# Six fixed experts and ten ordered ones in a two-layer decoder: the unit of four at sixth place, the embedding's input on GpSimd's queue, the order read where it is first used

## The chip, the cores and the metric

The kernel runs on one core of one Trainium2 chip. The metric is the device time of one execution in microseconds (us). TensorE (PE), VectorE (DVE), ScalarE (ACT), GpSimd (POOL) and SyncE (SP) each run their own instruction stream in order and meet at semaphores; 16 DMA engines move data between HBM and the core's SBUF.

## What is computed

A decoder trunk of two layers over 256 tokens of width 1024, all in float32. Each layer is a mixer (layer 0: differential attention beside retention; layer 1: forgetting attention), a LayerNorm, a mixture of 16 experts of which each token takes two out of one group of four, a second LayerNorm, and a gated embedding of a per-layer input `p`:

```python
for i in range(DEPTH):
    h = layer_norm(DEEPNORM_ALPHA * x + mix, ...)
    ffn = grouped_moe(h, router_w, moe_w_gate[i], moe_w_up[i], moe_w_down[i])
    h = layer_norm(DEEPNORM_ALPHA * h + ffn, ...)
    x = h + jax.nn.sigmoid(h @ ple_gate[i]) * (p[i] @ ple_proj[i])

def grouped_moe(...):
    for e in range(N_EXPERTS):
        a = jax.nn.silu(h @ w_gate[e]) * (h @ w_up[e])
        y = y + dense_gate[..., e:e + 1] * (a @ w_down[e])
```

The experts' weights are most of the bytes: 16 experts of 6.3 MB in each of two layers, 201 MB of the 249 MB that are read.

## The kernel before

**Weights as a stream.** Every weight matrix is cut into chunks of 128 x 2048 floats (1 MB). `PLAN` lists all 236 chunks in the order of their use; `fetch` issues the next chunk on SP's DMA queue, as two halves of 512 KB into the pool `wp` (36 halves), or into a place of its own where `PLACES` names one ("split": four quarters in the pool of the split weights; 0, 1, 2: one of the big activation slots; "late": a tile of the layer). A half is loaded again when the matmuls that read it are done, in the order of their use. SP's stream holds hardly anything but these issues, so it runs ahead of the other engines by as much as the buffers allow. Each DMA raises one of eight semaphores, taken in turn (`DMAHW0` to `DMAHW7`, called lanes below), and an issue waits until the DMA that had its lane before has landed; so about eight of SP's transfers are under way at a time, and a DMA that ACT issues takes its turn among the same eight lanes. GpSimd's DMAs have semaphores of their own (`DMASW`).

**Experts in units.** A token's rows are gathered for an expert into 64 slots. `UNITS` pairs the experts, so that two of them share the 128 columns of the array; one unit holds four experts with 32 slots each (`LIGHT`). The units are worked through in this order, each by its place p from 0 to 6: `gate_up(p)` (matmuls of L1305), `act`, then `down(p - 1)` (L1335) and `scatter(p - 1)` (L1355). Before p = 0, `rows` (L1243) gathers the tokens; again after every odd p.

**Ranked experts.** Experts 0 to 3 (`FIXED`) are read where they lie. The other twelve are ranked by their number of tokens: the eight fullest become experts 4 to 11 and the four lightest 12 to 15, the unit of four. DVE finds the ranks in `order`, `values_load` (L1166) loads them into twelve registers of SP, and every later address of such an expert is made of one of these registers. If any expert has more tokens than slots (64, or 32 in the unit of four), a flag `fi` is 1, all engines take the branch of L1471 and `overflow` runs every expert once more in a loop.

**What the change touches.** `moe_steps` writes out the expert part of `PLAN`; its last two lines move the two chunks of `u` of experts 2 and 3 behind six later ones. `pT`, the transposed input `p` of the layer, is loaded on ACT's queue (L1479) into a slot in which a chunk of an earlier unit lies (`PLACES` 59), and read by the matmuls of `pp` (L1430 and L1422). `router`, `order`, `later` and `back` hold the router's small DVE operations.

Of the kernel before, what the change touches and what calls it, by code (L numbers as in the profile page):

```python
# [10 lines left out]
F32 = mybir.dt.float32  # L11
# [4 lines left out]
U32 = mybir.dt.uint32  # L16
AF = mybir.ActivationFunctionType
OP = mybir.AluOpType
# [8 lines left out]
ALPHA = 4.0 ** 0.25  # L27
# [8 lines left out]
PPAT = 5  # L36


FIXED, LIGHT = 4, 32
UNITS = [(0, 1), (2, 3), (4, 5), (12, 13, 14, 15), (6, 7), (8, 9), (10, 11)]  # L40
LAST = len(UNITS) - 1
PLACES = {20: "split", 21: "split", **{j + i: n for j in (14, 37, 58) for i, n in enumerate((0, 1, "late"))}, 79: 0, 22: 2}

# [6 lines left out]
def moe_steps(l):  # L50
    def down(p, fh=(0, 1)):
        return [("d", l, e, h) for h in fh for e in UNITS[p]]

    out = []
    for p in range(len(UNITS)):
        out += [(n, l, e, kh) for n in ("g", "u") for kh in range(2) for e in UNITS[p]]
        if p == 1:

            out += down(0) + down(1)
        elif p > 2:  # L60
            out += down(p - 1)
        if p == PPAT:
            out.append(("pp", l, 0))
    for fh in range(2):
        out += down(LAST, (fh,))
        if l == DEPTH - 1 and fh == 0:
            out += EARLY
    out.append(("pp", l, 1))

    i = out.index(("u", l, 2, 1))  # L70
    return out[:i] + out[i + 2:i + 8] + out[i:i + 2] + out[i + 8:]
# [162 lines left out]
def trunk(ctx: ExitStack, tc, w, xT_d, pT_d, prm_d, rows_d, rb_d, cst_d, e_d, dt_d, out):  # L234
    nc = tc.nc
# [10 lines left out]
    def bank(tag, dt=F32):  # L246
        return psum.tile([128, 512], dt, name=tag, tag=tag)
# [3 lines left out]
    pos = [0]  # L251
# [8 lines left out]
    ranked = {}  # L260

    def source(key, c):

        if key[0] in ("g", "u", "d") and key[2] >= FIXED:
            l = key[1]
            of = w[(l * NE + FIXED) * 6:(l + 1) * NE * 6].rearrange("(x j) p c -> x j p c", j=6)
            return of[bass.ds(ranked[l][key[2] - FIXED], 1), "gud".index(key[0]) * 2 + key[3], :, c]
        return w[AT[key], :, c]

# [801 lines left out]
    def router(l, lt, rstd, finish, keep, residual, two):  # L1071
# [69 lines left out]
        NS = NE - FIXED  # L1141
        tmp = two.tile([128, 512], F32, name="r_tmp", tag="a", bufs=1)
        key = tmp[:, 0:32].rearrange("p (i e) -> p i e", i=2)
        perm = tmp[:, 32:176].rearrange("p (r e) -> p r e", r=NS)
        prod = tmp[:, 176:464].rearrange("p (t r e) -> p t r e", t=2, r=NS)
        load = tmp[:, 464:480]
        far = tmp[:, 480:496].rearrange("p (i r) -> p i r", i=2)
        rank = tmp[:, 496:512].bitcast(U32).rearrange("p (i r) -> p i r", i=2)
        spos = keep.tile([128, 2, 16], F32, name="r_spos")

        def arranged(out, in_):
# [5 lines left out]
        def order(behind):  # L1157

            with tc.issue_after(behind):
                DVE.tensor_copy(load, cnt)  # L1160
                DVE.scalar_tensor_tensor(key[:, 0, 0:NS], load[:, FIXED:], 16.0, i16[:, 0:NS], op0=OP.mult, op1=OP.subtract)
            DVE.tensor_scalar(key[:, 1, 0:NS], key[:, 0, 0:NS], -1.0, None, op0=OP.mult)
            for i in range(2):
                DVE.max(out=far[:, i, :], in_=key[:, i, 0:NS])
                DVE.max_index(out=rank[:, i, :], in_max=far[:, i, :], in_values=key[:, i, 0:NS])
            _, ranked[l] = nc.values_load_multi_w_load_instructions(  # L1166
                rank[0:1].rearrange("p i r -> p (i r)")[:, 0:NS], engines=[mybir.EngineType.SP], min_val=0, max_val=NS - 1,
                skip_runtime_bounds_check_because="indices of the largest of so many")
            DVE.tensor_tensor(perm, i16[:, None, 0:NS].to_broadcast([128, NS, NS]),
                              rank.rearrange("p i r -> p (i r)")[:, 0:NS, None].to_broadcast([128, NS, NS]), op=OP.is_equal)  # L1170
            arranged(spos, pos)

        def later():

            ri = new([2], "r_ri")
            DVE.reciprocal(ri, rs)
            pr = new([2, 2], "r_pr")
            DVE.tensor_tensor(pr, m8[:, :, 0:2], ri[:, :, None].to_broadcast([128, 2, 2]), op=OP.mult)
            gsum = new([2], "r_gsum")
            DVE.tensor_tensor(gsum, pr[:, :, 0], pr[:, :, 1], op=OP.add)  # L1180
            DVE.reciprocal(gsum, gsum)
            DVE.tensor_tensor(pr, pr, gsum[:, :, None].to_broadcast([128, 2, 2]), op=OP.mult)
            e2 = eq.rearrange("p t j e -> p (t j) e")
            DVE.tensor_tensor(e2, e2, pr.rearrange("p t j -> p (t j)")[:, :, None].to_broadcast([128, 4, 16]), op=OP.mult)
            gate = keep.tile([128, 2, 16], F32, name="r_gate")
            DVE.tensor_tensor(gate, eq[:, :, 0, :], eq[:, :, 1, :], op=OP.add)
            sgate = keep.tile([128, 2, 16], F32, name="r_sgate")
            DVE.tensor_copy(sgate[:, :, 0:FIXED], gate[:, :, 0:FIXED])
            arranged(sgate, gate)

            cap = keep.tile([128, 16], F32, name="r_cap")
            DVE.memset(cap, float(CAP))
            DVE.tensor_scalar(cap[:, FIXED:], key[:, 1, 0:NS], far[:, 1, 3:4], None, op0=OP.is_ge)
            DVE.tensor_scalar(cap[:, FIXED:], cap[:, FIXED:], float(LIGHT - CAP), float(CAP), op0=OP.mult, op1=OP.add)

            fm = small.tile([1, 16], F32, name="r_fm")
            DVE.tensor_tensor(fm, load[0:1], cap[0:1], op=OP.is_gt)
            fi = keep.tile([1, 1], I32, name="r_fi")
            DVE.tensor_reduce(fi, fm, axis=AX.X, op=OP.max)
            return gate, sgate, cap, fi  # L1200

        return pos, spos, order, later, rest


    def moe(l, hT, n2, acc, keep, two, xs, residual, *lt):
            pos, spos, order, later, rest = router(l, *lt, keep, residual, two)
            gate = sgate = cap = fi = None
            g0, b0 = P_MG + 8 * l, P_MB + 8 * l
            xg, sl, aT, sT, gsl = {}, {}, {}, {}, {}
            last = []  # L1210
# [43 lines left out]

            def back(q, after=None):

                nonlocal gate, sgate, cap, fi
                if q == 0:
                    with tc.issue_after(after):
                        gate, sgate, cap, fi = later()  # L1260
                s32 = two.tile([128, 2, 4 * CAP], F32, name="sel", tag="a", bufs=1)
                select(q, s32)
                o = bank("w").rearrange("p (b t) -> p b t", b=2)
                og = bank("w")
                us = UNITS[2 * q:2 * q + 2]
                for b in range(len(us)):
                    for tt in range(2):
                        c = slice(b * 128, (b + 1) * 128)
                        PE.transpose(o[:, b, tt * 128:(tt + 1) * 128], s32[:, tt, c], ident)
                        PE.matmul(og[:, 16 * b:16 * b + 16], lhsT=s32[:, tt, c], rhs=sgate[:, tt, :],  # L1270
                                  start=tt == 0, stop=tt == 1, skip_group_check=True)
                st = two.tile([128, 2, 256], FR, name="sT")
                DVE.tensor_copy(st[:, 0:len(us)], o[:, 0:len(us)])
                sT[q] = st

                gg = two.tile([128, 2], F32, name="gg")
                if len(together(q)) < len(us):
                    for i in range(2):
                        r, c = slice(64 * i, 64 * i + 64), us[0][i]
                        DVE.tensor_scalar(gg[r], og[r, c:c + 19:18], 1.0 / ALPHA, None, op0=OP.mult)  # L1280
                else:
                    for b, es in enumerate(us):
                        n = 128 // len(es)
                        for i, e in enumerate(es):
                            r = slice(n * i, n * i + n)
                            DVE.tensor_scalar(gg[r, b:b + 1], og[r, 16 * b + e:16 * b + e + 1], 1.0 / ALPHA, None, op0=OP.mult)
                gsl[q] = gg

            def gate_up(p, between, amid=None):
# [70 lines left out]
            def overflow():  # L1360

                T = two.tile
                og = T([128, 2, 16], F32, name="og", tag="og", bufs=1)
                DVE.tensor_tensor(og, pos, cap[:, None, :].to_broadcast([128, 2, 16]), op=OP.is_gt)
                DVE.scalar_tensor_tensor(og, og, 1.0 / ALPHA, gate, op0=OP.mult, op1=OP.mult)
                id16 = T([128, 128], F16, name="id16", tag="id16", bufs=1)
                DVE.tensor_copy(id16, ident)

# [83 lines left out]
            for p in range(len(UNITS)):  # L1452
# [23 lines left out]
                    gb = broadcast()  # L1476
                if p == PPAT:
                    pT = slot(XSLOT[l][1], "pT", shape=(128, 2, S))
                    nc.scalar.dma_start(out=pT, in_=pT_d[l])  # L1479
                    ppT = keep.tile([128, 8, S], F32, name="ppT", tag="late")  # L1480
                    for o in pp(0, pT, ppT):
                        DVE.tensor_scalar(*o, 0.5, None, op0=OP.mult)
# [140 lines left out]
```

## Time and profile before

| | us |
|---|---|
| median of three runs | 758.33 |
| lowest and highest | 757.03 and 761.68 |
| the profiled execution's own time | 759.22 |
| span of its instructions | 757.2 |

The span is counted from the first to the last instruction of the program in the one execution that was profiled; 2.0 us of that execution's time lie around it. Its time is 0.9 us above the median. Times inside the profile are us from the start of the span. Of the engines, PE is busy for 95% of the span, DVE 42%, ACT 32%, POOL 6%; PE's busy time is modelled, so that a matmul that waits between its parts can look busy.

### The profile page before, as it was taken

To read this page: it belongs to the slowest core of one execution; us is meant where nothing else is said; L and a number is where in the kernel's file an instruction comes from. 1 tells how busy PE (TensorE), PEld (TensorE's weight loads), DVE (VectorE), ACT (ScalarE), POOL (GpSimd) and SP (SyncE) were. 2 spreads that over 40 slices of the span, in tenths; PEclk is the share of its full clock that TensorE was granted. 3 is DMA by queue.
4 is the path that set the end of the run, shared out by engine and by line. 5 is a ranking of instruction groups with operands and counts; after the bars stand their busy time and mean duration, and the time that the engine had idled before them with its cause. 6 is when DMAs were issued, how large, how long until landed. Compare 5 with 4: busy or idle time off the path is not lost. (4 is left out here: it accounts for less than half of the span.)

```text
span 757.2 us, 11670 instructions
## 1 busy us (share of the span) xinstructions
PE 718.0 (95%) x4126; PEld 426.9 (56%) x4126; DVE 321.0 (42%) x799; ACT 242.3 (32%) x507; POOL 44.5 (6%) x42
## 2 busy tenths in 40 slices
PE   6999999999999897999999999989999998799897
PEld 6977887435334232547989897763443432243367
DVE  6687777303102011218757666671221211020585
ACT  5557656101001010105667566451111100020441
POOL 3000101000000000004000000010000000000036
PEclk9999999999999999999999999999999999999999
DMA  8999883899999799999997437559999969999901
GB/s 285 376 408 408 325 295 123 329 410 415 407 409 414 255 409 409 408 403 409 408 410 289 137 141 281 187 179 371 413 411 409 414 247 344 407 409 409 395 37 56
DMA packets 70526, 250.82 MB, mean 331 GB/s; under 512 B 7835, under 2 KB 9408, under 8 KB 67776
## 3 DMA queue, kind: packets, MB, share of 16 engines
q1 hardware_dynamic: 70176, 249.51, 84.8%
q8 instruction: 34, 0.56, 0.3%
q10 hardware_dynamic: 288, 0.52, 0.3%
q14 instruction: 28, 0.23, 0.1%
HBM read 248.95 MB, written 1.05 MB: 330 GB/s over the span
## 5 line engine op out<-in xcount | busy, mean ns | idle before, releaser
L1305 PE MATMUL w<-wt,xg 128*64 128x512 f32 (+1 forms) x1024 | 204.3, 595 | 7.5 <-DMA wt<-in_w_dram 5.1
L1335 PE MATMUL w<-wt,aT 128*64 128x512 f32 (+1 forms) x512 | 129.8, 607 | 15.6 <-DMA wt<-in_w_dram 15.5
L1305 PEld LDWEIGHTS w<-wt,xg 128*64 128x64 f32 (+1 forms) x1024 | 63.3, 130 | 130.0 <-issue 106.4
L385 DVE TENSOR_TENSOR wlo<-wt,whi 128x512 fp32r<-128x512 f32 x145 | 106.4, 749 | 42.6 <-ACT whi L383 35.3
L383 ACT ACTIVATE whi<-wt 128x512 fp32r<-128x512 f32 x148 | 91.0, 629 | 63.4 <-PE acc L435 24.9
L1335 PEld LDWEIGHTS w<-wt,aT 128*64 128x64 f32 (+1 forms) x512 | 39.5, 132 | 96.6 <-issue 63.5
L1346 ACT ACTIVATE whi<-w,gg 128x512 fp32r<-128x512 f32 x28 | 19.3, 688 | 184.9 <-PE w L1335 166.4
L1312 DVE TENSOR_TENSOR a<-a,w 128x512 f32<-128x512 f32 x14 | 9.6, 687 | 140.8 <-PE w L1305 101.8
L435 PE MATMUL acc<-xh,whi 128*128 128x256 f32 x192 | 50.9, 290 | 5.4 <-ACT whi L383 5.4
L1347 DVE SCALAR_TENSOR_TENSOR wlo<-w,gg,whi 128x512 fp32r<-128x512 f32 x28 | 20.6, 746 | 73.0 <-ACT whi L1346 72.8
L435 PE MATMUL acc<-xh,wlo 128*128 128x256 f32 x192 | 50.7, 289 | 0.8 <-DVE wlo L385 0.8
L1311 ACT ACTIVATE a<-w 128x512 f32<-128x512 f32 x14 | 8.4, 597 | 119.0 <-PE w L1305 57.7
L435 PEld LDWEIGHTS acc<-xh,whi 128*128 128x128 f32 x192 | 37.4, 196 | 6.7 <-ACT whi L383 6.5
L377 POOL TENSOR_TENSOR lnrs<-lnve,mhalf 128x1 f32<-128x1 f32 x8 | 4.4, 546 | 589.3 <-DVE lnve L467 586.1
L435 PEld LDWEIGHTS acc<-xh,wlo 128*128 128x128 f32 x192 | 37.4, 195 | 1.5 <-DVE wlo L385 1.3
L421 PE MATMUL acc<-whi,xh 128*128 128x512 f32 x96 | 38.1, 396 | 0.0
L421 PE MATMUL acc<-whi,xl 128*128 128x512 f32 x96 | 38.0, 396 | 0.0
L421 PE MATMUL acc<-wlo,xh 128*128 128x512 f32 x96 | 37.1, 390 | 0.0
L435 PE MATMUL acc<-xl,whi 128*128 128x256 f32 x192 | 37.1, 286 | 0.0
L1253 ACT ACTIVATE xg<-w,prm 128x256 f32<-128x256 f32 (+1 forms) x32 | 15.5, 534 | 63.3 <-PE w L1243 63.2
L1320 DVE COPY aT<-w 128x512 f32<-128x512 f32 x14 | 9.7, 692 | 53.4 <-PE w L1335 40.0
L435 PEld LDWEIGHTS acc<-xl,whi 128*128 128x128 f32 x192 | 29.5, 195 | 0.0
(314 smaller groups left out, 1008.0 us busy)
## 6 DMA issues: line engine op xcount, KB each, us to landing
wt<-in_w_dram SPq DMA_DIRECT2D x406, 512.0 KB, 10.1
wt<-in_w_dram SPq DMA_DIRECT2D x21, 1024.0 KB, 10.9
wt<-in_w_dram SPq DMA_DIRECT2D x40, 256.0 KB, 5.7
x<-in_xT_dram SPq DMA_DIRECT2D x3, 256.0 KB, 5.8
dt<-in_dt_dram SPq DMA_DIRECT2D x1, 512.0 KB
tmp<-scr SPq DMA_DIRECT2D x1, 512.0 KB, 6.2
pT<-in_pT_dram ACTq DMA_DIRECT2D x2, 256.0 KB, 2.7
out_dram<-wt SPq DMA_DIRECT2D x2, 256.0 KB, 2.0
```

The costliest lines, as they stand in the source:

```text
L383: i = ACT.activation(hi, src, AF.Copy)
L385: return i, (eng or DVE).tensor_tensor(lo, src, hi, op=OP.subtract)
L421: PE.matmul(o, lhsT=wa[p], rhs=wb[q], start=start and i == 0, stop=stop and i == 2, skip_group_check=True)
L435: m = PE.matmul(outs[b], lhsT=ws[kk][i % 2][:, b * 128:(b + 1) * 128], rhs=x2[i // 2][:, kk, :], start=kk == 0 and b in first and i == 0, ...
L1253: ACT.activation(xt[:, k, 0:n], o[:, b, :], AF.Identity, bias=be, scale=g)
L1305: PE.matmul(o[m * i:m * i + m, :], lhsT=xg[p // 2][:, k, c:c + m], rhs=ws[i, k // 4][k % 4], start=k == 0, stop=k == 7)
L1311: ACT.activation(a, ps["g"], AF.Silu)
L1312: DVE.tensor_tensor(a, a, ps["u"], op=OP.mult)
L1320: DVE.tensor_copy(t.rearrange("p f s -> p (f s)"), pt)
L1335: PE.matmul(ob[nh][m * i:m * i + m, :], lhsT=aT[p][:, f, m * i:m * i + m], rhs=ws[i, f // 2][2 * (f % 2) + nh], start=f == 0, stop=f == 3)
L1346: last[:] = (ACT.activation(yh, ob[nh], AF.Copy, scale=gg), DVE.scalar_tensor_tensor(yl, ob[nh], gg, yh, op0=OP.mult, op1=OP.subtract))
L1347: DVE.scalar_tensor_tensor(yl, ob[nh], gg, yh, op0=OP.mult, op1=OP.subtract))
```

## The change

`FIXED` is 6 instead of 4, so ten experts are ranked: the six fullest of them are experts 6 to 11, the four lightest 12 to 15. The unit of four stands sixth (p = 5) instead of fourth (p = 3). `moe_steps` lists every unit's `d` chunks one unit later, from the first on, as `down` uses them. The registers of SP are loaded by a function that runs when the first ranked expert's address is made. The ranks get a tile of their own (`r_rank`), `cap` a corner of the temporary one, and the overflow's gate is made in `later` and no longer in the branch. `pT` is loaded on GpSimd's queue.

```diff
-FIXED, LIGHT = 4, 32
-UNITS = [(0, 1), (2, 3), (4, 5), (12, 13, 14, 15), (6, 7), (8, 9), (10, 11)]
+FIXED, LIGHT = 6, 32
+UNITS = [(0, 1), (2, 3), (4, 5), (6, 7), (8, 9), (12, 13, 14, 15), (10, 11)]
...
-        if p == 1:
-
-            out += down(0) + down(1)
-        elif p > 2:
+        if p:
             out += down(p - 1)
...
+            if callable(ranked[l]):
+                ranked[l] = ranked[l]()
             return of[bass.ds(ranked[l][key[2] - FIXED], 1), "gud".index(key[0]) * 2 + key[3], :, c]
...
-        perm = tmp[:, 32:176].rearrange("p (r e) -> p r e", r=NS)
-        prod = tmp[:, 176:464].rearrange("p (t r e) -> p t r e", t=2, r=NS)
+        perm = tmp[:, 32:32 + NS * NS].rearrange("p (r e) -> p r e", r=NS)
+        prod = tmp[:, 176:176 + 2 * NS * NS].rearrange("p (t r e) -> p t r e", t=2, r=NS)
...
-        rank = tmp[:, 496:512].bitcast(U32).rearrange("p (i r) -> p i r", i=2)
+        rank = keep.tile([128, 16], U32, name="r_rank")
...
-                DVE.max_index(out=rank[:, i, :], in_max=far[:, i, :], in_values=key[:, i, 0:NS])
-            _, ranked[l] = nc.values_load_multi_w_load_instructions(
-                rank[0:1].rearrange("p i r -> p (i r)")[:, 0:NS], engines=[mybir.EngineType.SP], min_val=0, max_val=NS - 1,
-                skip_runtime_bounds_check_because="indices of the largest of so many")
+                DVE.max_index(out=rank[:, i * (NS - 4):i * (NS - 4) + 8], in_max=far[:, i, :], in_values=key[:, i, 0:NS])
+            ranked[l] = lambda: nc.values_load_multi_w_load_instructions(
+                rank[0:1, 0:NS], engines=[mybir.EngineType.SP], min_val=0, max_val=NS - 1,
+                skip_runtime_bounds_check_because="indices of the largest of so many")[1]
...
+            DVE.tensor_copy(spos[:, :, 0:FIXED], pos[:, :, 0:FIXED])
             arranged(spos, pos)
...
-            cap = keep.tile([128, 16], F32, name="r_cap")
+            cap = tmp[:, 496:512]
...
-            return gate, sgate, cap, fi
+
+            beyond = prod.rearrange("p t r e -> p (t r e)")[:, 0:32].rearrange("p (t e) -> p t e", t=2)
+            DVE.tensor_tensor(beyond, pos, cap[:, None, :].to_broadcast([128, 2, 16]), op=OP.is_gt)
+            DVE.scalar_tensor_tensor(gate, beyond, 1.0 / ALPHA, gate, op0=OP.mult, op1=OP.mult)
+            return gate, sgate, fi
...
                 if p == PPAT:
                     pT = slot(XSLOT[l][1], "pT", shape=(128, 2, S))
-                    nc.scalar.dma_start(out=pT, in_=pT_d[l])
+                    nc.gpsimd.dma_start(out=pT, in_=pT_d[l])
```

Where the instructions stand is seen in the built programs. On SP's queue, at layer 0's expert part, the quarters `128x512` are the chunks of `u` of experts 2 and 3, `TENSOR_LOAD` is the load of the registers, and an `ISA` row makes an address from one. Before:

```order
L290 DMA wt<-in_w_dram 128x1024 x46
L290 DMA wt<-in_w_dram 128x2048 x3
L290 DMA wt<-in_w_dram 128x1024 x6
L290 DMA wt<-in_w_dram 128x512 x4
L1166 TENSOR_LOAD r_tmp
L290 DMA wt<-in_w_dram 128x512 x4
L290 DMA wt<-in_w_dram 128x2048
L290 DMA wt<-in_w_dram 128x1024 x2
L290 ISA
L290 DMA wt<-in_w_dram 128x1024
```

After the change, the same place:

```order
L289 DMA wt<-in_w_dram 128x1024 x46
L289 DMA wt<-in_w_dram 128x2048 x3
L289 DMA wt<-in_w_dram 128x1024 x6
L289 DMA wt<-in_w_dram 128x512 x8
L289 DMA wt<-in_w_dram 128x2048
L289 DMA wt<-in_w_dram 128x1024 x18
L1165 TENSOR_LOAD r_rank
L289 ISA
L289 DMA wt<-in_w_dram 128x1024
```

The load of the registers has moved behind 23 issues: the second four quarters, one chunk in a slot, and 18 halves.

On ACT's queue in layer 0, `pT` stands behind the `a` of the unit at p = 4 (with what each instruction waits for). Before:

```order
L1346 ACTIVATE whi<-w,gg 128x512 [waits PE_49] x2
L1253 ACTIVATE xg<-w,prm 128x256 [waits PE_49]
L1253 ACTIVATE xg<-w,prm 128x256
L1311 ACTIVATE a<-w 128x512 [waits DVE_49,PE_49]
L1479 DMA pT<-in_pT_dram 128x512 [waits DMAHW5_49,DMAHW7_49,DMAHW4_49,PE_49]
L1346 ACTIVATE whi<-w,gg 128x512 [waits PE_49,Activation_49] x2
```

After the change it stands on POOL's queue, behind the branch of the overflow and ahead of the LayerNorm's small operations:

```order
L1472 ISA [waits DMASW3_49,DMASW4_49,DMASW2_49,DMASW5_49,DMASW1_49,DMASW0_49]
L1472 UNCONDITIONAL_BRANCH
L1480 DMA pT<-in_pT_dram 128x512 [waits DMAHW5_49,DMAHW4_49,DMAHW7_49,DMASW0_49,PE_49]
L376 TENSOR_TENSOR lnrs<-lnve,mhalf 128x1 [waits DVE_49,Activation_49,Pool_49]
L376 TENSOR_TENSOR lnrs<-lnve,mhalf 128x1 [waits DVE_49]
```

It waits for PE's last read of its slot, as before, and its landing is told by a semaphore of GpSimd's (`DMASW0`).

On PE, at the end of layer 0's expert part, the last unit's `gate_up` is followed by the `down` of the unit before it. `64x512` are matmuls of a pair, `32x512` of the unit of four. Before:

```order
L1430 MATMUL w<-pT,wt 128x256 x8
L1305 MATMUL w<-wt,xg 64x512 x16
...
L1305 MATMUL w<-wt,xg 64x512 x16
L1335 MATMUL w<-wt,aT 64x512 x16
L1318 MATMUL w<-identr,a 128x128 x4
L1355 MATMUL acc<-whi,sT 128x512 x2
```

After the change:

```order
L1431 MATMUL w<-pT,wt 128x256 x8
L1309 MATMUL w<-wt,xg 64x512 x9
...
L1309 MATMUL w<-wt,xg 64x512 x16
L1339 MATMUL w<-wt,aT 32x512 x2
L1322 MATMUL w<-identr,a 128x128 x4
L1339 MATMUL w<-wt,aT 32x512 x30
L1359 MATMUL acc<-whi,sT 128x512 x2
```

The `down` that PE meets there is now that of the unit of four, which reads eight chunks instead of four.

## Rows read from the trace of the kernel before

**Rows 1.** The page: the GB/s that the DMA engines moved in 40 equal slices of the span (18.9 us each).

```profile
GB/s 285 376 408 408 325 295 123 329 410 415 407 409 414 255 409 409 408 403 409 408 410 289 137 141 281 187 179 371 413 411 409 414 247 344 407 409 409 395 37 56
```

**Rows 2.** The chain of work that ended last, merged: start, us, what. The last transfer in it, of layer 1's expert part.

```profile
704.72 9.53 DMA wt<-in_w_dram
```

**Rows 3.** PE in order of time: start, us, line, operation, tiles, shapes, number of instructions (two to a matmul in float32), and in brackets the idle time before and what ended it. The first expert matmul of each layer; then of layer 0 a half of `gate_up` and a `down` of a pair, `gate_up` and a part of `down` of the unit of four, and the last `down`; then the last `down` of layer 1.

```profile
131.96 1.51 PE L1305 MATMUL w<-wt,xg 128*64 128x512 f32 x6 [0.50 <-ACT xg L1253]
506.22 1.08 PE L1305 MATMUL w<-wt,xg 128*64 128x512 f32 x4 [0.50 <-ACT xg L1253]
...
177.14 7.09 PE L1305 MATMUL w<-wt,xg 128*64 128x512 f32 x32
192.33 7.04 PE L1335 MATMUL w<-wt,aT 128*64 128x512 f32 x32
202.93 13.93 PE L1305 MATMUL w<-wt,xg 128*32 128x512 f32 x126
261.86 6.39 PE L1335 MATMUL w<-wt,aT 128*32 128x512 f32 x24 [2.53 <-DMA wt<-in_w_dram]
334.98 8.11 PE L1335 MATMUL w<-wt,aT 128*64 128x512 f32 x30
714.29 7.31 PE L1335 MATMUL w<-wt,aT 128*64 128x512 f32 x16 [2.99 <-DMA wt<-in_w_dram]
```

**Rows 4.** Waits of SP's queue over the whole span: who waited for whom, us in total, times, the longest.

```profile
SPq L290 <- DMA pT<-in_pT_dram: 26.2, 2, 14.8
SPq L290 <- PE w L1305: 24.1, 44, 5.5
SPq L1166 <- DVE r_tmp L1165: 20.7, 2, 12.9
```

**Rows 5.** SP's queue in order of time, from four windows that hold two issues each: start of the first, us from there to the end of the second, line, tile, number of issues. Layer 0, layer 0, layer 1, layer 1.

```profile
118.50 14.91 SPq L290 DMA_DIRECT2D wt<-in_w_dram  x2
242.34 12.22 SPq L290 DMA_DIRECT2D wt<-in_w_dram  x2
498.06 10.47 SPq L290 DMA_DIRECT2D wt<-in_w_dram  x2
609.89 15.70 SPq L290 DMA_DIRECT2D wt<-in_w_dram  x2
```

**Rows 6.** The same view. The first two run from each layer's first expert weight over 124 issues; the other three over 24 issues of 512 KB or as many bytes: an undisturbed stretch, then layer 0 and layer 1 from the first issue of the second and fourth of rows 5.

```profile
49.02 193.65 SPq L290 DMA_DIRECT2D wt<-in_w_dram  x124
383.30 226.93 SPq L290 DMA_DIRECT2D wt<-in_w_dram  x124
199.14 29.70 SPq L290 DMA_DIRECT2D wt<-in_w_dram  x24
242.34 35.99 SPq L290 DMA_DIRECT2D wt<-in_w_dram  x24
609.89 39.90 SPq L290 DMA_DIRECT2D wt<-in_w_dram  x24
```

**Rows 7.** The view of the tile `pT`, over both layers: ACT's issue of its DMA (the times of the two issues stand behind the durations in ns), and the time from issue to landing.

```profile
L1479 ACTq DMA_DIRECT2D pT<-in_pT_dram x2: 339/358/377, 251.3 to 622.5; - x2
DMA to landing us min/median/max: 2.6/2.7/2.8
```

**Rows 8.** PE by line from 251.2 to 343.1, which is layer 0's expert part from the last read of the slot that `pT` takes: line, operation, tiles, shapes, number of instructions, busy us and mean ns of one, idle us before them and what ended it. The three groups that are left out are busy for 0.6 us or less each.

```profile
L1335 PE MATMUL w<-wt,aT 128*64 128x512 f32 (+1 forms) x160 | 39.2, 614 | 6.8 <-DMA wt<-in_w_dram 6.7
L1305 PE MATMUL w<-wt,xg 128*64 128x512 f32 x129 | 30.0, 596 | 3.0 <-DMA wt<-in_w_dram 2.2 <-PEq L1471 0.7
L1355 PE MATMUL acc<-whi,sT 128*128 128x512 f32 x13 | 4.7, 432 | 0.1
L1355 PE MATMUL acc<-wlo,sT 128*128 128x512 f32 x12 | 4.1, 429 | 0.0
L1430 PE MATMUL w<-pT,wt 128*128 128x256 f32 x16 | 3.7, 384 | 0.0
L1318 PE MATMUL w<-identr,a 128*128 128x128 f32 x12 | 2.0, 287 | 0.0
L1243 PE MATMUL w<-sel,n 128*128 128x128 f16 x32 | 2.0, 219 | 0.0
```

**Rows 9.** Stretches of 10 us: PE, PEld, DVE, ACT and POOL busy (instructions), the granted TensorE clock, the DMA engines' busy share, GB/s. Four of layer 0's expert part, one of layer 1's.

```profile
120.00:130.00 10.00, 8.95 (x93) 7.40 (x92) 7.00 (x36) 8.33 (x22) 2.84 (x3) 1.00 0.16 51
250.00:260.00 10.00, 9.23 (x50) 2.34 (x45) 0.69 (x1) 0.00 (x0) 0.00 (x0) 1.00 0.58 179
260.00:270.00 10.00, 8.02 (x29) 2.58 (x30) 1.71 (x3) 1.38 (x2) 0.00 (x0) 0.83 1.01 398
280.00:290.00 10.00, 7.31 (x32) 2.24 (x32) 0.64 (x1) 0.00 (x0) 0.00 (x0) 1.00 1.03 408
620.00:630.00 10.00, 9.77 (x53) 2.77 (x50) 0.69 (x1) 0.00 (x0) 0.00 (x0) 1.00 0.45 141
```

**Rows 10.** DVE in order of time in layer 0's router: the last index search, one of the four large operations of `arranged`, and the selection that PE waits for.

```profile
131.66 0.17 DVE L1165 FIND_INDEX8 r_tmp<-r_tmp 128x8 uint32<-128x12 f32 x1
134.30 0.45 DVE L1153 TENSOR_TENSOR r_tmp<-r_tmp,r_gate 128x288 f32<-128x288 f32 x1
135.28 0.76 DVE L1229 TENSOR_TENSOR sel<-stay,r_pos 128x256 f32<-128x256 f32 x2
```

More of the change, by code (lines that the diff above doesn't have):

```diff
@@ L1164, in order @@
                 DVE.max(out=far[:, i, :], in_=key[:, i, 0:NS])
-                DVE.max_index(out=rank[:, i, :], in_max=far[:, i, :], in_values=key[:, i, 0:NS])
-            _, ranked[l] = nc.values_load_multi_w_load_instructions(
-                rank[0:1].rearrange("p i r -> p (i r)")[:, 0:NS], engines=[mybir.EngineType.SP], min_val=0, max_val=NS - 1,
-                skip_runtime_bounds_check_because="indices of the largest of so many")
+                DVE.max_index(out=rank[:, i * (NS - 4):i * (NS - 4) + 8], in_max=far[:, i, :], in_values=key[:, i, 0:NS])
+            ranked[l] = lambda: nc.values_load_multi_w_load_instructions(
+                rank[0:1, 0:NS], engines=[mybir.EngineType.SP], min_val=0, max_val=NS - 1,
+                skip_runtime_bounds_check_because="indices of the largest of so many")[1]
             DVE.tensor_tensor(perm, i16[:, None, 0:NS].to_broadcast([128, NS, NS]),
-                              rank.rearrange("p i r -> p (i r)")[:, 0:NS, None].to_broadcast([128, NS, NS]), op=OP.is_equal)
+                              rank[:, 0:NS, None].to_broadcast([128, NS, NS]), op=OP.is_equal)
+            DVE.tensor_copy(spos[:, :, 0:FIXED], pos[:, :, 0:FIXED])
             arranged(spos, pos)
@@ L1206, in moe @@
             pos, spos, order, later, rest = router(l, *lt, keep, residual, two)
-            gate = sgate = cap = fi = None
+            og = sgate = fi = None
             g0, b0 = P_MG + 8 * l, P_MB + 8 * l
@@ L1255, in back @@
             def back(q, after=None):
-                nonlocal gate, sgate, cap, fi
+                nonlocal og, sgate, fi
                 if q == 0:
                     with tc.issue_after(after):
-                        gate, sgate, cap, fi = later()
+                        og, sgate, fi = later()
                 s32 = two.tile([128, 2, 4 * CAP], F32, name="sel", tag="a", bufs=1)
@@ L1263, in back @@
                 o = bank("w").rearrange("p (b t) -> p b t", b=2)
-                og = bank("w")
+                sg = bank("w")
                 us = UNITS[2 * q:2 * q + 2]
@@ L1269, in back @@
                         PE.transpose(o[:, b, tt * 128:(tt + 1) * 128], s32[:, tt, c], ident)
-                        PE.matmul(og[:, 16 * b:16 * b + 16], lhsT=s32[:, tt, c], rhs=sgate[:, tt, :],
+                        PE.matmul(sg[:, 16 * b:16 * b + 16], lhsT=s32[:, tt, c], rhs=sgate[:, tt, :],
                                   start=tt == 0, stop=tt == 1, skip_group_check=True)
@@ L1279, in back @@
                         r, c = slice(64 * i, 64 * i + 64), us[0][i]
-                        DVE.tensor_scalar(gg[r], og[r, c:c + 19:18], 1.0 / ALPHA, None, op0=OP.mult)
+                        DVE.tensor_scalar(gg[r], sg[r, c:c + 19:18], 1.0 / ALPHA, None, op0=OP.mult)
                 else:
@@ L1285, in back @@
                             r = slice(n * i, n * i + n)
-                            DVE.tensor_scalar(gg[r, b:b + 1], og[r, 16 * b + e:16 * b + e + 1], 1.0 / ALPHA, None, op0=OP.mult)
+                            DVE.tensor_scalar(gg[r, b:b + 1], sg[r, 16 * b + e:16 * b + e + 1], 1.0 / ALPHA, None, op0=OP.mult)
                 gsl[q] = gg
@@ L1362, in overflow @@
                 T = two.tile
-                og = T([128, 2, 16], F32, name="og", tag="og", bufs=1)
-                DVE.tensor_tensor(og, pos, cap[:, None, :].to_broadcast([128, 2, 16]), op=OP.is_gt)
-                DVE.scalar_tensor_tensor(og, og, 1.0 / ALPHA, gate, op0=OP.mult, op1=OP.mult)
                 id16 = T([128, 128], F16, name="id16", tag="id16", bufs=1)
```

## The prediction

> **What bounds the kernel now.** I read the DMA engines' GB/s by slices first, then the chain that ended last, then SP's waits, and last PE inside the expert parts. An undisturbed stream moves 408 to 414 GB/s; inside the expert parts there are dips that no other engine's work explains: 123 in the slice from 114 us, 255 from 246, 247 from 606 [rows 1]. The chain ends in weight transfers, and behind the last of them PE's last `down` starts after 2.99 us of waiting for it [rows 2, 3]. PE looks busy, but from 251.2 to 343.1 in layer 0 its work is four `down` at 7.04 (28.2), four halves of `gate_up` at 7.09 (28.4) [rows 3], and shorter groups of 16.5 plus at most 1.8 [rows 8]: 74.9 of 91.9 us, so 17.0 us are waits, whole or inside matmuls. In layer 1 the same work lies between 622.5 [rows 7] and 714.29 + 7.31 = 721.6 [rows 3]: 99.1 us, so 24.2 us of waits. The weight stream sets the end of both expert parts, and a hole in it comes back there us for us until these 17 and 24 us are used up. A hole's owner is read from SP: it waited 12.9 us for the register load, up to 14.8 us for `pT`, and 44 times for PE, 5.5 us at most [rows 4].
>
> **The register load.** In layer 0 two neighbouring issues of SP take 14.91 us from 118.50 on [rows 5]; between them stands the load, which waits for the index search that ends at 131.83 [rows 10]. Meanwhile the stream falls to 51 GB/s [rows 9]. Behind the load stand three chunks whose places are free (the second four quarters and two others), 3.1 MB, 7.7 us at 408 GB/s: the most that can be won. A second count: the first 124 issues of the expert part end at 242.67 in layer 0, 110.71 us after PE's first expert matmul, and at 610.23 in layer 1, 104.01 us after it [rows 3, 6]. In layer 1 the load's hold (10.47 us, to 508.53) ends where PE starts to free buffers, just after 506.22 [rows 3, 5], so it costs nothing there. The difference, 6.7 us, is what the load costs layer 0; I take it, between 0 and 7.7, since it is measured on the same 124 issues. After the change the load stands 23 issues later; the ranks are long known there, and the load with one issue takes 1.6 us (131.83 to 133.41), with eight transfers of 29.70/23 = 1.29 us under way [rows 6]: nothing. So **−6.7 us, in layer 0 alone**.
>
> **`pT`.** On ACT's queue its DMA takes one of eight lanes in program order, but is issued only when PE has read its slot, at 251.3 and 622.5 [rows 7]; the SP issue next on that lane waits for it. Two issues take 12.22 and 15.70 us [rows 5], and the stream falls to 179 and 141 GB/s [rows 9]. Over 24 issues that is 35.99 and 39.90 us against 29.70 [rows 6]: 6.3 and 10.2 us, of which `pT`'s own 256 KB (0.64 us at 408 GB/s) stay. On GpSimd's queue it has a semaphore that no SP instruction waits for: **−5.7 us in layer 0, −9.6 in layer 1**. The bounds are zero and the full 6.3 and 10.2. These holds end with PE and not with the stream, so layer 1's lead of 6.7 us is eaten by a hold that is 3.5 us longer; undoing one hold alone would therefore be worth less than its share.
>
> Is there cover? In layer 0, 6.7 + 5.7 = 12.4 come off 17.0 us of PE's waits, 4.6 are left; in layer 1, 9.6 off 24.2, 14.6 are left. Next late is the stream again.
>
> GpSimd's transfer is not in this trace. ACT's landed in 2.6 to 2.8 us [rows 7]. In the new order the slot is freed in the middle of p = 5's first half, and PE wants `pT` at `pp(0)`, about half a `gate_up` half, one more, a `down`, transposes, scatter and the gather later: 3.5 + 7.1 + 7.0 + some 5 = 23 us, which is hidden at 2.7 us and up to 23. I take zero. ACT waits for nothing of `pT`, so there is no gain beside the lane. On POOL behind it stand only the LayerNorm's small operations at the layer's end.
>
> **The unit of four at sixth place.** Its PE work is a pair's: 13.93 us against 2 x 7.09 [rows 3]. Its weights are 24 chunks (25 MB) where a pair's are 12, 61 us of stream. What moves is where PE waits for them: its `down` (eight chunks, 20.5 us of stream, 7 us of PE) now stands just ahead of the last `down`, so PE meets a lump of some 6 to 8 us of waits at the end. What that costs is the clock: a wait of 2.53 us in the four's `down` came with a granted clock of 0.83 over its 10 us, while 280 to 290, where PE was busy for 7.31 of 10 in many short waits, had 1.00 [rows 3, 9]. 0.83 is 3.4 us at the lower level (1.2 GHz) in ten, 1.7 us of work lost; it counts only behind the last transfer of an expert part. Bounds: the last `down`s took 8.11 for 30 instructions and 7.31 for 16, against 6.6 and 3.5 at 0.22 each [rows 3], so if the new order took their waits away, −1.5 and −3.8; if each layer loses what that dip cost and 0.7 of a gap more, +2.4. In layer 1 three chunks of `ppg` (7.7 us) stand between the lump and the last `down` and cover it. I take half the upper figure for layer 0 and zero for layer 1, nearest to the 0.83 row: **+1.2 us**.
>
> [...]
>
> **Router and the rest.** In place of operations on 288 elements (0.45 us each, four of them [rows 10]) stand such on 200, and a small copy and two small operations are added at about 0.17 each, the last two behind the selection: between −0.5 and +0.5, taken as zero. The overflow's gate leaves a branch that isn't taken. Buffers are freed in the order of use as before; `d` is now listed a unit later from the first on, so that SP waits for PE at other issues. It waited 44 times already [rows 4] and the slices from 530 to 606 still show 411 to 414 GB/s [rows 1]: eight transfers under way (10.3 us) cover a wait of 5.5. Zero, with the rival below.
>
> **Sum** on the profiled execution: 759.2 − 6.7 − 5.7 − 9.6 + 1.2 = 738.4; that execution is 0.9 above the median, so **737.5 us**. With every term at its better end (7.7, 6.3, 10.2, −5.3) it is 728.8, with every one at its dearer end, short of a rival, some 744. A difference within 1% (7.6 us) cannot be told from none by a measurement of this kernel.
>
> **Rivals.** *PE becomes the bound in layer 0.* Only 4.6 us of its waits are left by the sum. If the lump stands at the lower clock for longer (a `down` at half speed is 7 us dearer in each layer; layer 1's cover takes most of its), the time is 737.5 + 7 = 744 to 748. For it: 0.83 and 2.5 us waits already; against it: at most one such dip in a stretch now. Chance 0.12.
>
> *SP waits for PE instead.* With `d` listed later, issues wait for reads by PE that themselves wait for weights. If one wait in each layer outlasts the 10.3 us under way by the longest seen, 5.5 [rows 4], the time is 737.5 + 11 = 748. Against it: the full slices from 530 on. Chance 0.05.
>
> *The change doesn't do what it says:* the stream still halts for `pT`. Then layer 0's lead of 6.7 us is eaten at the hold as in layer 1, and the time is the old one with the four's cost, 757 to 760. The holes are waits with idle DMA engines (share 0.45 to 0.58 [rows 9]), and the program shows no SP issue on GpSimd's semaphore. Chance 0.04.
>
> The Trainium skill ("DMA: Bandwidth & Descriptors", section "Rules for kernel authors") says that spreading DMAs over SP, ACT and GpSimd brings no bandwidth, since all run on the same 16 engines, and only saves issue time. By that alone `pT` would be worth nothing and the time would be this rival's; the idle share in the rows says that the gain here is an order of waiting, not bandwidth.
>
> *Slower:* `pT` by GpSimd comes late. PE then stands at `pp(0)`, in order ahead of p = 6. The 23 us of cover and the waits left (4.6 and 14.6) hide it up to 28 and 38 us; each us beyond is paid. At 47 us it is 19 + 9 = 28 more, 766, slower by 1%. No row speaks for a 256 KB transfer of 47 us; the nearest is 2.7. Chance 0.03.
>
> **Numbers.** The forecast has 0.76, in 730 to 744. With the two rivals of 0.12 and 0.05 in part, the range **730 to 747** holds a little over 8 in 10. Faster by over 1% (below 750.7): 0.76 + 0.12 + 0.04 less some doubt in all of them, **0.87**; within 1%: **0.09**; slower: **0.04**.
>
> **What would show it.** In the changed profile SP has no wait of 12 us or more in either expert part except for PE; the first 124 issues end about 104 us after the first expert matmul in both layers; GB/s stays near 408 from 140 to the end of layer 0's weights; its last `down` ends near 332 instead of 343.1; `pT` is issued by POOL and PE doesn't wait for it; PE's waits for weights lie in the four's `down` with a clock below 1.00 there; the span is some 736. Wrong would be: a new hole of the stream with PE behind SP's waits, a wait of PE for `pT`, or a last `down` that starts long after its weights have landed.

## The result and the profile after

The changed kernel takes 734.79 us (median of four runs, 732.79 to 737.25) beside 758.66 for the kernel before: ratio 0.968, 95% interval 0.964 to 0.9725. The profiled execution is the longest of the four, 737.25 us with a span of 735.4; it stands against 759.22 and 757.2.

The page of the changed kernel, engines' busy time and GB/s by slices (18.4 us each):

```profile
PE 711.4 (97%) x4126; PEld 427.8 (58%) x4126; DVE 320.7 (44%) x805; ACT 242.4 (33%) x507; POOL 45.8 (6%) x44
...
GB/s 287 354 410 408 371 263 261 322 389 415 410 408 414 408 407 410 408 377 401 409 408 301 128 141 282 185 189 333 412 413 409 412 411 408 406 410 408 391 4 58
```

Of the three dips of [rows 1], two are gone: the slices that answer to 255 and 247 show 408 to 414. The third is shallower, 261 where it was 123. The lower slices from 74 to 147 us, around the start of the expert part, stay. Waits of SP's queue, whole span: who waited for whom, us in total, times, the longest.

```profile
SPq L289 <- PE w L1309: 64.9, 52, 9.5
SPq L289 <- PE w L1339: 17.6, 23, 3.6
```

Against [rows 4] the lines for `pT` and for the register load are missing, and the waits for PE's reads in `gate_up` have grown from 24.1 to 64.9 us, the longest from 5.5 to 9.5. SP's first 124 issues from each layer's first expert weight, as in [rows 6]: start, us, line, tile, number.

```profile
49.77 185.53 SPq L289 DMA_DIRECT2D wt<-in_w_dram  x124
372.67 224.81 SPq L289 DMA_DIRECT2D wt<-in_w_dram  x124
```

And PE in order of time, as in [rows 3]: the first expert matmul of each layer, layer 0's last `down`, layer 1's.

```profile
132.04 3.65 PE L1309 MATMUL w<-wt,xg 128*64 128x512 f32 x16 [0.50 <-ACT xg L1257]
493.93 3.65 PE L1309 MATMUL w<-wt,xg 128*64 128x512 f32 x16 [0.50 <-ACT xg L1257]
...
323.19 8.11 PE L1339 MATMUL w<-wt,aT 128*64 128x512 f32 x30
691.81 8.39 PE L1339 MATMUL w<-wt,aT 128*64 128x512 f32 x16 [3.22 <-DMA wt<-in_w_dram]
```

The 124 issues now end 103.3 us (235.30 − 132.04) and 103.6 us (597.48 − 493.93) after the first expert matmul; before it was 110.7 and 104.0. From the first expert matmul to the end of the last `down`, layer 0 takes 199.3 us where it took 211.1, and layer 1 takes 206.3 where it took 215.4. These two stretches hold 21.0 of the 21.8 us that the span lost.

### The profile page after: what moved, and what is told of

Read it like the earlier page. It is cut to its first block, busy times and chain, and to the rows that moved or that the text cites. A ratio compares the mean times of both kernels' runs of the same rounds, so it can differ in the third digit from the quotient of the medians.

```text
span 735.4 us, 11580 instructions
## 1 busy us (share of the span) xinstructions
PE 711.4 (97%) x4126; PEld 427.8 (58%) x4126; DVE 320.7 (44%) x805; ACT 242.4 (33%) x507; POOL 45.8 (6%) x44
## 4 chain that ended last, share of the span: by engine, by line
PE 76%; DMA 18%; DVE 3%; ACT 2%; issue 1%; POOL 0%; SPq 0%; DVEq 0%; ACTq 0%; POOLq 0%
PE w L1309 21%; DMA wt<-in_w_dram 18%; PE acc L420 13%; PE acc L434 13%; PE w L1339 11%; PE w L1247 3%; PE acc L1553 2%; PE acc L1359 2%; PE w L962 1%; PE w L1008 1%; PE w L1322 1%; PE w L1553 1%; DVE lnst L458 1%; PE w L622 1%; PE w L782 1%
## 5 line engine op out<-in xcount | busy, mean ns | idle before, releaser
L1339 PE MATMUL w<-wt,aT 128*64 128x512 f32 (+1 forms) x512 | 123.5, 604 | 3.7 <-DMA wt<-in_w_dram 3.5
L1247 PE MATMUL w<-sel,n 128*128 128x256 f16 (+1 forms) x256 | 28.1, 260 | 2.6 <-ACT xg L1257 1.8
```

Source lines behind the costliest of these rows:

```text
L1247: PE.matmul(os[kb][:, b, :], lhsT=n2[j][:, tt, k * 128:(k + 1) * 128], rhs=sel[:, tt, 0:n], start=b == 0 and i == 0, stop=i == 3, skip_gro ...
L1339: PE.matmul(ob[nh][m * i:m * i + m, :], lhsT=aT[p][:, f, m * i:m * i + m], rhs=ws[i, f // 2][2 * (f % 2) + nh], start=f == 0, stop=f == 3)
```

## Experiments

Each kernel's stretches are read as above, from its first expert matmul and the end of its last `down` in each layer; "rest" is what is left of the span. The time is the median of the runs, the ratio that to the kernel before in the same runs.

| kernel | time, us | ratio (95%) | layer 0 | layer 1 | rest |
|---|---|---|---|---|---|
| before | 758.66 | | 211.1 | 215.4 | 330.7 |
| changed | 734.79 | 0.968 (0.964 to 0.9725) | 199.3 | 206.3 | 329.9 |
| pt_alone | 742.7 | 0.9785 (0.9769 to 0.9801) | 205.3 | 205.9 | 329.7 |
| load_alone | 758.66 | 1.0001 (0.9991 to 1.0012) | 212.2 | 214.2 | 330.2 |
| pt_and_load | 735.68 | 0.9687 (0.9669 to 0.9705) | 199.6 | 204.6 | 330.2 |
| units_back | 734.89 | 0.969 (0.9667 to 0.9714) | 198.0 | 204.5 | 329.6 |
| pt_back | 745.29 | 0.981 (0.9783 to 0.9837) | 202.8 | 211.8 | 329.9 |
| load_back | 735.08 | 0.9681 (0.9658 to 0.9703) | 199.1 | 205.7 | 329.5 |
| load_in_tmp | 739.07 | 0.9731 (0.9711 to 0.9751) | 203.2 | 205.7 | 329.8 |
| after_again | 734.48 | 0.967 (0.9654 to 0.9687) | 198.2 | 204.7 | 329.9 |
| pg_last | 733.37 | 0.9664 (0.9647 to 0.9681) | 198.3 | 198.2 | 335.3 |
| pg_last_again | 733.36 | 0.9661 (0.9644 to 0.9678) | 197.6 | 198.2 | 335.3 |
| pg_one | 733.49 | 0.9666 (0.9649 to 0.9684) | 197.9 | 199.6 | 334.3 |
| old_order_pg_last | 735.34 | 0.9689 (0.9669 to 0.9708) | 198.1 | 198.6 | 335.8 |

**pt_alone**, the kernel before with one line changed:

```diff
-                    nc.scalar.dma_start(out=pT, in_=pT_d[l])
+                    nc.gpsimd.dma_start(out=pT, in_=pT_d[l])
```

> The kernel before with one edit: pT is loaded on GpSimd's queue. Theory (holes in the weight stream come back us for us): the holds of 12.2 and 15.7 us in SP's queue are gone, 5.7 and 9.6 us less, the register load's hole of 6.7 us in layer 0 stays: 743 us beside 758.5 of before, ratio 0.980. Rival (the stream's halt is not what sets the end of the expert parts, PE's own work is): 755 or more.

742.7, with 5.8 us gone in layer 0 and 9.4 in layer 1. SP has no wait for `pT` any more; the hole at the register load stays:

```profile
SPq L1166 <- DVE r_tmp L1165: 20.3, 2, 12.9
```

**load_alone**, the changed kernel with these lines put back and `pT` on ACT's queue:

```diff
-FIXED, LIGHT = 6, 32
-UNITS = [(0, 1), (2, 3), (4, 5), (6, 7), (8, 9), (12, 13, 14, 15), (10, 11)]
+FIXED, LIGHT = 4, 32
+UNITS = [(0, 1), (2, 3), (4, 5), (12, 13, 14, 15), (6, 7), (8, 9), (10, 11)]
...
-        if p:
+        if p == 1:
+            out += down(0) + down(1)
+        elif p > 2:
             out += down(p - 1)
```

> The changed kernel with the six fixed experts, the old order of units, the old order of the weights and pT on ACT's queue put back to before (four fixed, four-expert unit fourth): of the change only the register load at first use and the overflow's gate outside the branch are left. Theory: the 6.7 us that the weight stream wins in layer 0 are eaten at the hold for pT, which ends with PE's read and not with the stream; time within 1.5 us of before, SP's hold for pT in layer 0 some 6 us longer (about 18). Rival (each part is worth its own share, wherever the other stands): 752 us, ratio 0.991.

758.66, ratio 1.0001. SP's wait for `pT`:

```profile
SPq L292 <- DMA pT<-in_pT_dram: 32.1, 2, 17.6
```

The two neighbouring issues of SP between which it stands in layer 0 (start, us, line, tile, number):

```profile
235.76 18.51 SPq L292 DMA_DIRECT2D wt<-in_w_dram  x2
```

The view of the tile `pT` in the same kernel, ACT's issues (durations in ns, then the start of the first and the last):

```profile
L1483 ACTq DMA_DIRECT2D pT<-in_pT_dram x2: 339/358/376, 251.1 to 623.1; - x2
```

SP reaches the place at 235.8 instead of 242.3, but leaves it at the same time (254.27; before 254.56 [rows 5]), since PE frees the slot at the same time: `pT` is issued at 251.1, before at 251.3 [rows 7]. The lead is lost whole: this kernel issues the three chunks ahead of the register load, as the changed kernel does, and is no faster.

**pt_and_load** is that kernel with `pT` on GpSimd's queue.

> The changed kernel with only the six fixed experts, the units' order and the weights' order put back to before: pT on GpSimd's queue and the register load at first use stay. Theory: both holes gone, 22.0 us less, 736.5; so that the order of units would be worth between -2 and +2 us beside the changed kernel's 734.8. Rival (the place of the four-expert unit carries part of the gain): 740 or more.

735.68. The register load, worth nothing beside the `pT` hold, is worth 7.0 us (742.7 to 735.68) once that hold is gone; the two together are worth 23.0, and the place of the four, the six fixed experts and the order of the weights hardly anything here.

**units_back**, one line of the changed kernel:

```diff
-UNITS = [(0, 1), (2, 3), (4, 5), (6, 7), (8, 9), (12, 13, 14, 15), (10, 11)]
+UNITS = [(0, 1), (2, 3), (4, 5), (12, 13, 14, 15), (6, 7), (8, 9), (10, 11)]
```

> The changed kernel with the unit of four back at fourth place and nothing else put back. Theory: no hole comes back; PE meets the four's waits for weights in the middle and not ahead of the last down; 733 to 737 us, the wait of 3.2 us ahead of layer 1's last down is still there, since the three chunks of the gate's weights stand between. Rival (the late place is what hides the four's 61 us of stream): 740 or more.

734.89: no difference beyond the spread of the runs, and the wait ahead of layer 1's last `down` is still there:

```profile
689.81 7.03 PE L1339 MATMUL w<-wt,aT 128*64 128x512 f32 x16 [2.98 <-DMA wt<-in_w_dram]
```

**pt_back**, the changed kernel with the line of pt_alone put back.

> The changed kernel with pT back on ACT's queue. Theory: SP halts again in each layer until PE has read the slot, and layer 0's lead goes with it as in the kernel with the register load alone: 22 us dearer, 757, ratio to before about 0.998. Rival (each part is worth its share): 5.7 and 9.6 dearer, 750.

745.29, below both theories: 10 us dearer than the changed kernel, not 22 and not 15. SP's wait:

```profile
SPq L289 <- DMA pT<-in_pT_dram: 17.1, 2, 9.0
```

The two issues around it in layer 0 and in layer 1:

```profile
254.57 9.89 SPq L289 DMA_DIRECT2D wt<-in_w_dram  x2
...
621.87 8.95 SPq L289 DMA_DIRECT2D wt<-in_w_dram  x2
```

The view of the tile `pT` in the same kernel, ACT's issues:

```profile
L1480 ACTq DMA_DIRECT2D pT<-in_pT_dram x2: 347/364/382, 259.1 to 624.5; - x2
```

In load_alone SP came to the lane 15.3 us before the slot was free (235.8 against 251.1); here 4.5 us before (254.6 against 259.1), and in layer 1 2.6 us before (621.9 against 624.5). The rest of each hold is the transfer of `pT` itself. `pT` is issued when PE frees its slot, as my theory says, but the new orders let SP reach the place later in its stream. I had taken the hold's length from the old order and carried it over. So the six fixed experts and the two new orders together do bring something: they make a halt for `pT` half as dear (10 us here, 23 from pt_and_load to load_alone), which with `pT` on GpSimd's queue is not needed. Which of the three does it was not run.

**load_back** was to put the register load back where the ranks are made:

```diff
-            ranked[l] = lambda: nc.values_load_multi_w_load_instructions(
+            _, ranked[l] = nc.values_load_multi_w_load_instructions(
```

> The changed kernel with the register load back where the ranks are made, pT still on GpSimd's queue. Theory: the hole of layer 0 between 119 and 133 us is back and nothing eats it: 6.7 dearer than the changed kernel, 741.5, ratio to before 0.977; layer 1 as in the changed kernel.

735.08, as the changed kernel. The reason is in the built program: on all five engines it has the same instructions in the same order as the changed kernel. The call at first use moves nothing here. What lets the load stand later is that the ranks have a tile of their own; my reading is that with the shared tile its next writers have to wait until the load has read it.

**load_in_tmp** is load_back with the tiles exchanged, too:

```diff
-        rank = keep.tile([128, 16], U32, name="r_rank")
+        rank = tmp[:, 496:512].bitcast(U32)
...
-            cap = tmp[:, 496:512]
+            cap = keep.tile([128, 16], F32, name="r_cap")
```

> The changed kernel with the register load made where the ranks are made and the ranks back in the shared temporary tile (cap in a tile of its own instead); pT on GpSimd's queue and the new orders stay. Unlike with the load alone moved back, its instruction now stands ahead of two quarters, a chunk in a slot and 18 halves in SP's stream again. Theory: SP waits at the index search of layer 0 to 133 us as before the change, the hole costs up to 6.7: 738 to 742 us; layer 1 as in the changed kernel. Rival (in the new order the issues behind the load have to wait for PE anyway): 735.

On SP's queue the load now stands ahead again of two quarters, a chunk in a slot and 18 halves:

```
L289 DMA wt<-in_w_dram 128x512 x6
L1165 TENSOR_LOAD r_tmp
L289 DMA wt<-in_w_dram 128x512 x2
L289 DMA wt<-in_w_dram 128x2048
L289 DMA wt<-in_w_dram 128x1024 x18
```

739.07, 4.6 us above the changed kernel in the same runs (734.48), and layer 0 is longer, by 3.9 to 5.1; layer 1 lies between the two traces of the changed kernel. SP's wait in this kernel:

```profile
SPq L1165 <- DVE r_tmp L1164: 8.4, 1, 8.4
```

Its stretches of 10 us from 120 on, with the columns of [rows 9]:

```profile
120.00:130.00 10.00, 8.94 (x93) 7.38 (x91) 6.99 (x37) 8.21 (x22) 2.83 (x3) 1.00 0.30 104
130.00:140.00 10.00, 9.50 (x60) 4.76 (x59) 7.45 (x39) 2.04 (x4) 0.00 (x0) 1.00 0.47 169
```

Before, the wait was 12.9 us [rows 4] and the first stretch showed 51 GB/s [rows 9]: here the load stands behind two more quarters, SP comes to it later and waits 8.4 us, and the hole costs less than 6.7.

**pg_last** and **pg_one** take up the wait of 3.2 us that is left ahead of layer 1's last `down`. `EARLY` lists the chunks of the gate's weights that are loaded between the two halves of that `down`'s weights, and split on ACT and DVE ahead of it.

```diff
-EARLY = [("pg", DEPTH - 1, 0, 0), ("pg", DEPTH - 1, 0, 1), ("pg", DEPTH - 1, 1, 0)]
+EARLY = []
```

> The changed kernel with the list of the gate's weights that are loaded and split ahead of layer 1's last down emptied, so that all four chunks of them come behind it, as in layer 0. Theory: the wait of 3.2 us ahead of the second half of layer 1's last down and the low clock behind it come from these three chunks (7.7 us of stream), so both are gone and the last down ends about 7 us earlier; against that, twelve more splits of a quarter chunk (0.75 us each on DVE) fall behind the last down: 731 to 738. Rival (the wait comes from the unit of four ahead of it): the wait stays, over 738.

pg_one keeps the first of the three.

> As the kernel that loads the gate's weights last, but one of the three chunks stays ahead of the last down. Theory: 2.6 us of stream stand between, which PE's backlog covers; the wait is about nothing, four splits of a quarter are done early and eight late: 730 to 736, at or below the changed kernel. Rival as there.

733.37 and 733.49. In pg_last and pg_one the last `down` of layer 1 has no idle time before it; of pg_last_again, the same kernel, the rows of that `down`:

```profile
679.41 1.07 PE L1339 MATMUL w<-wt,aT 128*64 128x512 f32 x2
681.99 8.11 PE L1339 MATMUL w<-wt,aT 128*64 128x512 f32 x30
```

The stretches from 690 on in the same kernel:

```profile
690.00:700.00 10.00, 8.84 (x36) 5.19 (x36) 9.59 (x19) 6.74 (x14) 4.82 (x5) 1.00 0.67 258
700.00:710.00 10.00, 8.98 (x38) 6.75 (x38) 9.96 (x11) 4.29 (x8) 7.57 (x5) 1.00 0.00 0
```

In the changed kernel the same place, 690 to 700:

```profile
690.00:700.00 10.00, 8.19 (x16) 2.40 (x16) 3.05 (x5) 2.67 (x5) 0.00 (x0) 0.66 0.88 330
```

Layer 1's expert part is 6.5 to 8.1 us shorter, the clock stays at 1.00, and 5.4 of it are given back behind it, where DVE is now busy for 9.6 to 10 of 10 us with the splits and PE waits for them. In pg_last_again:

```profile
PE acc L1553 <- DVE wlo L384: 3.3, 4, 1.7
```

So behind the last `down` the bound has gone from the stream to DVE, as I read it.

**after_again**, **pg_last_again** and **old_order_pg_last** were run on one chip; the last is pt_and_load with `EARLY` empty.

> The changed kernel once more, on the chip of the next two. Both theories: 734 to 736, with some 4 us between its runs.

> The kernel that loads the gate's weights of layer 1 behind the last down, once more. Theory: the low clock behind the wait of 3 us is what makes the changed kernel's runs differ; without it the runs lie within 1 us, and 1 to 2 us below the changed kernel. Rival (the difference was the chip's): within 0.5 us of it.

> As the one before, but with four fixed experts, the old order of units and the old order of the weights. Theory: with both holes gone and no wait ahead of layer 1's last down, neither the place of the unit of four nor the six fixed experts are worth anything: within 1 us of it. Rival (the forecast's cost of 1.2 us for a wait of PE at the end of layer 0): 1 us or more faster.

734.48, 733.36 and 735.34. Loading the gate's weights last is 1.1 us faster here; pg_last was 1.4 below the first measurement of the changed kernel and 1.7 below load_back, the same program, in the same runs. But the intervals of the ratios overlap here (0.9654 to 0.9687 and 0.9644 to 0.9678), so I call it the fastest kernel that was run and no more. That the runs of the changed kernel differ because of the clock doesn't hold: on this chip its five runs lie within 0.6 us (734.06 to 734.65), those of pg_last_again within 1.4. The old order is 2.0 us behind the new one, which neither theory had, though these two intervals touch as well (0.9669 to 0.9678); it is 0.4 to 0.5 us longer in each stretch of the trace, and with the gate's weights in their place the two orders came out alike (734.89 and 735.68 against 734.79). What makes the 2.0 stays open.

## Why the prediction was right, and where it was not

The forecast was 737.5 us, in 730 to 747; 734.79 was measured. On the profiled execution it was 738.4, and 737.25 was measured. Point by point:

- **What bounds the kernel.** The stream did: taking holes out of it shortened both expert parts and nothing else (rest 330.7 to 329.9).
- **`pT`**: 5.7 and 9.6 us forecast; pt_alone gave 5.8 and 9.4. The count of 24 issues against an undisturbed stretch was exact to 0.2 us.
- **The register load**: 6.7 us; 7.0 by the times of pt_alone and pt_and_load, 5.7 by layer 0's stretch in their traces. The comparison of the two layers over 124 issues was the right one. That the lead is lost at a hold that ends with PE was argued from layer 1 and is shown by load_alone. The prediction took the load's new place from the built program and named no cause; the change was made as if the call at first use did it. load_back and load_in_tmp show that it is the tile of its own.
- **The unit of four**: +1.2 us in layer 0, for a lump of 6 to 8 us of waits with a low clock behind it. This term failed. The changed kernel's PE at that place, the last half of `gate_up` and the four's `down`; SP's 16 issues of that `down`'s eight chunks; a half's median time from issue to landing on the page; two stretches with the columns of [rows 9]:

```profile
301.12 7.09 PE L1309 MATMUL w<-wt,xg 128*64 128x512 f32 x32
308.14 1.90 PE L1339 MATMUL w<-wt,aT 128*32 128x512 f32 x4
310.56 5.37 PE L1339 MATMUL w<-wt,aT 128*32 128x512 f32 x40
316.19 3.62 PE L1339 MATMUL w<-wt,aT 128*32 128x512 f32 x20 [0.27 <-DMA wt<-in_w_dram]
...
287.40 20.23 SPq L289 DMA_DIRECT2D wt<-in_w_dram  x16
...
wt<-in_w_dram SPq DMA_DIRECT2D x406, 512.0 KB, 10.1
...
310.00:320.00 10.00, 9.73 (x66) 3.18 (x66) 0.15 (x1) 0.84 (x2) 0.00 (x0) 1.00 1.02 407
320.00:330.00 10.00, 9.88 (x38) 4.03 (x38) 1.86 (x3) 0.54 (x1) 0.00 (x0) 1.00 0.98 353
```

  This `down` takes 11.7 us (308.14 to 319.81) with 0.7 us of transposes in it, for 7 us of work. So about 4 us are lost, 0.27 as an idle engine and the rest while PE counts as busy; the prediction's 6 to 8 has no working. The clock, which is what the term charged for, stayed at 1.00 from 240 to 330, the last `down` takes 8.11 us as before [rows 3], and units_back shows no cost of the place. The step at fault is the reading of PE's backlog. I set the eight chunks' 20.5 us of stream against 7 us of PE, and left out that PE works on the last unit's `gate_up` from 292 to 308, while those chunks land, by the rows above, from about 298 to 317: half of them are there when the `down` starts.
- **Layer 1's cover.** I counted the three chunks of the gate's weights as cover for the last `down`. They are transfers ahead of its second half, and so the cause of its wait, before [rows 3] as after: 2.99 and 3.22 us; with the list emptied it is gone, in the new order (pg_last) and in the old (old_order_pg_last). It was nothing that the change did, so the sum did not suffer.
- **SP waits for PE instead**: it does, 82.5 us (64.9 + 17.6) with the longest of 9.5. The time shows no loss, and in the middle of both expert parts the slices stay at 406 to 415 GB/s; the longest wait is still below the 10.3 us that eight transfers take.
- **The rival in which the stream still halts for `pT`** was priced at 757 to 760. pt_back puts it at 745.3: the price was wrong, since the hold's length belongs to the orders in the stream and not to `pT` alone.
- **`pT` by GpSimd**: wanted 28.9 us after its issue (259.7 to 288.6; 23 forecast), landed after 6.3 to 7.3; no wait of PE, as forecast. The view of the tile in the changed kernel:

```profile
L1431 PE MATMUL w<-pT,wt x32: 377/379/463, 288.6 to 336.9; 128*128 128x256 f32 x32
...
L1480 POOL DMA_DIRECT2D pT<-in_pT_dram x2: 585/664/742, 259.7 to 621.7; - x2
...
DMA to landing us min/median/max: 6.3/6.8/7.3
```

- **The router's operations**: the selection starts at 135.42 in layer 0, 135.28 before [rows 10]; zero, as taken.
- **The range.** Its dearer end before rivals, "some 744", has no working: with the bounds that stand beside the terms (zero for the load and for both holds of `pT`, +2.4 in each layer) it would be 763.
- **The signs.** The 124 issues end 103.3 and 103.6 us after the first expert matmul (104 forecast), layer 0's last `down` ends at 331.3 (332), the span is 735.4 (736). The clock below 1.00 in the four's `down` did not come.

The median is 2.7 us below the forecast. 1.2 is the term of the four; the rest lies within what the runs of the changed kernel differ by (732.79 to 737.25).

The Trainium skill's rule that spreading DMAs over the engines' queues brings no bandwidth ("DMA: Bandwidth & Descriptors", section "Rules for kernel authors") is not contradicted: the full slices show some 410 GB/s before and after. The 15 us of pt_alone come from what waited, which the rule doesn't speak of.

## What to carry to other kernels

Look for a transfer that shares a set of semaphores, in program order, with a long stream, and itself waits for a compute engine: the stream waits with it, and a lead that it won before is lost there as far as it brings the stream to that place before the engine is done: all of it in load_alone, a part in pt_back. Two holes in a row are not worth the sum of their parts one by one: the first is worth nothing (1.0001) until the second is gone, then 7 us. Where a scheduler orders the instructions, ask which tile's next use holds an instruction early, rather than where the call is written.

## What the runs showed of the hardware

A load of 256 KB took 6.3 to 7.3 us from issue to landing on GpSimd's queue, with the stream at full rate beside it, 0.6 to 0.7 us of it POOL's issue; on ACT's queue it took 2.6 to 2.8 us, in the hole that it had made [rows 7]. Most of that difference is not the queue's. In pt_back, where SP comes to the place a few us before and transfers are still under way, the issue of SP that waits for ACT's load ends 5.4 and 6.3 us after that load was issued (254.57 + 9.89 against 259.1, 621.87 + 8.95 against 624.5), and a load of that size by SP itself, in the changed kernel's page, took 5.8 us:

```profile
wt<-in_w_dram SPq DMA_DIRECT2D x40, 256.0 KB, 5.8
```

A wait of PE of 3.22 us ahead of layer 1's last `down` came with a granted clock of 0.66 in the 10 us from 690 in one execution of the changed kernel, and one of 3.21 us with 0.83 in another; the 16 instructions behind it took 8.39 and 7.09 us. That `down` in after_again:

```profile
690.38 7.09 PE L1339 MATMUL w<-wt,aT 128*64 128x512 f32 x16 [3.21 <-DMA wt<-in_w_dram]
```

The stretch of 10 us that holds it:

```profile
690.00:700.00 10.00, 9.48 (x25) 3.78 (x26) 3.83 (x7) 2.21 (x4) 0.00 (x0) 0.83 0.75 285
```

So what the same wait costs differs by over 1 us from execution to execution. Nor is the longer wait the dearer one. The same `down` in pt_and_load and in load_in_tmp:

```profile
692.85 6.34 PE L1342 MATMUL w<-wt,aT 128*64 128x512 f32 x16 [2.97 <-DMA wt<-in_w_dram]
...
695.05 8.38 PE L1339 MATMUL w<-wt,aT 128*64 128x512 f32 x16 [2.86 <-DMA wt<-in_w_dram]
```
